# A decoder layer on one core: the samples' decode moved from the chunk loop into the last twelve projection pairs, with q, k and gates stored by chunk

## The chip, the cores and the metric

One Trainium2 chip, one of its cores. The metric is the device time of one execution, in microseconds. Engines: PE is TensorE, DVE is VectorE, ACT is ScalarE, POOL is GpSimd, SP is SyncE, which issues all the DMAs of this kernel.

## The reference

One step of a decoder layer (D = 1024) on 1024 prompt positions and on 8 samples of one position each, all in float32:

```python
x = layer_norm(ALPHA * x + 0.5 * swiglu(x, ffn1_wi, ffn1_wo), ln_g[0], ln_b[0])
z = x @ w_in + b_in
# z is split into q, k, v, o, i, f, B, C, h, gate_a, gate_b; k is scaled by 1/16
h, C, n, m = mlstm_chunkwise(q, k, v, log_i, log_f, C0, n0, m0)   # 4 heads of 256
y_a = (head_norm(h) * sigmoid(o)) @ w_a
y_b = (B * short_conv(C * h)) @ w_b
mix = (sigmoid(gate_a) * y_a + sigmoid(gate_b) * y_b) @ w_mix
x = layer_norm(ALPHA * x + mix, ln_g[1], ln_b[1])
# then a second swiglu with its norm, and a gated per-layer input with its norm
```

The prompt starts from a zero state and runs as eight chunks of 128 positions. Each sample has a state of its own, state_C of 4 heads x 256 x 256: one step of decode is C_new = w C + k v^T, numerator q C_new, denominator q n, both for each of 8 samples and 4 heads; C_new is an output. So the decode reads and writes 8 MB of state.

## The kernel before

All columns (1024 prompt, 8 samples) lie side by side as four blocks of 258: 256 prompt columns, then two samples. A wide matrix product is taken in three float32r products (high weight by high activation, high by low, low by high), with weights of 128x128 and moving tiles of 128x258.

The stages in order of time: the first feed-forward (to some 760 us), the norm, the projections (to some 1509 us), the chunk stage (1500 to 1880 us), the mixing product, the second feed-forward, the gated input.

**Projections.** `pair` (lines 388 to 425) takes 256 output rows by seven products of half-size operands in place of eight. Each product is 12 matmuls for each of two column halves; weights are combined ahead on POOL and DVE and cast by ACT (lines 226 to 243). Its outputs come through a callback `out`: DVE writes a block of 258 columns of d at line 402, 417, 418 or 422, the second index of d telling which of two tiles of 128 rows. `lin` calls it for one head (256 rows) of one of q, k, v, o, gate_b and gate_a. After the whole pair it applies the bias and activation to 1032 columns of each tile in one ACT instruction (line 850), for o a second one with the norm's gain (line 852), and stores the tile to DRAM (line 858). `sg_pair` gives two tiles d in turn from four buffers, so that the pair after can write while the store before runs. The order of calls is convolution, q, k, v of each head, then twelve pairs: o of four heads, gate_b of four, gate_a of four.

**Chunk stage.** For each chunk of 128 positions: scores of 4 heads by transposed operands (lines 1009 and 1017 on PE), state products (lines 157 to 159), the state's update, scaled by ACT at line 1022, the numerator on ACT and DVE (lines 1030 and 1034), its norm over 256 columns on DVE and POOL (lines 981 to 991) and its transposes (line 1059). `chunk_load` (lines 959 to 965) reads q, k and o from DRAM in pieces of 128 columns, 512 bytes each. Work that does not depend on chunks fills it: pieces of w_b and w_a products, with gate data read back at lines 1143 and 1152.

**Decode.** Four steps of one head stand in each chunk. A step (lines 1096 to 1107) loads 256 KB of state into one of two buffers (line 1100), loads v spread over partitions (line 1101), scales the state on ACT (line 1102), adds k v^T in two DVE instructions (line 1104), takes two matmuls into the PSUM tile pn (line 1105, 8 rows of 256) and stores the state (line 1107). After four steps `dec_end` (lines 1109 to 1119) copies pn, normalises it, transposes it and multiplies by the gate. `dec_start` prepares q spread over 8x8 columns (qd) and k scaled (kws).

**Order.** Each engine works through its own list of instructions in order. A scheduler sets the lists from the program's order and its own simulation; the ring of weight tiles and the PSUM tiles (four mm, three aux, one pn) limit how far an engine can run ahead. All DMAs go through SP's one list.

Of the kernel before, what the change touches and what calls it, by code (L numbers as in the profile page):

```python
# [56 lines left out]
def layer_kernel(ctx: ExitStack, tc: tile.TileContext, I, O):  # L57
# [520 lines left out]
    def tail1(RT, last):  # L578
# [10 lines left out]
    x2scr, qscr, kscr, oscr, yscr, ascr, bscr, tbscr, yfscr = (tc.dram_tile([8, 128, NT], F32, name=n) for n in (  # L589
        "x2scr", "qscr", "kscr", "oscr", "yscr", "ascr", "bscr", "tbscr", "yfscr"))  # L590
# [5 lines left out]
    count = {"sg": 0, "w": 0}  # L596
# [318 lines left out]

    conv(0, w0)
    lin(qscr, Q0, 0, AF.Identity, sm=0)
    lin(kscr, K0, 0, AF.Identity, 1.0 / 16.0, 1)
    val(0)
    gates()  # L920
    for h in range(1, 4):
        conv(h)
        lin(qscr, Q0, h, AF.Identity, sm=0)
        lin(kscr, K0, h, AF.Identity, 1.0 / 16.0, 1)
        val(h)
    for h in range(4):
# [3 lines left out]
    for h in range(4):  # L930
        lin(ascr, GA0, h, AF.Sigmoid)


    r_ = ring["slots"][ring["i"] % 9:] + ring["slots"][:ring["i"] % 9]
    big = [i for i in r_ if i in ("e0", "e1", "w4", "w5")]
    small = [i for i in r_ if i not in big]
    set_ring([big[0], small[0], big[1], small[1]])
    QH, QL, KH, KL = ((gen(i, R)[:, :D].rearrange("p (m n) -> p m n", n=128)) for i in small[2:5] + big[2:3])
    EP = gen(big[3])[:, :D]
    S_ = sreg()  # L940
    num = S_[:, 0:NT].rearrange("p (h e) -> p h e", e=258)
    P = S_[:, NT:NT + 512]
    qd = S_[:, NT + 512:NT + 1024].rearrange("p (h t a b) -> p h t a b", h=4, t=2, b=8)
    npc = S_[:, NT + 1024:NT + 1032]
    QC, KC, OC = ([gen(i)[:, :D].rearrange("p (m n) -> p m n", n=128) for i in ii] for ii in ((31, 27), (32, 8), (24, 35)))
    VH, VL = ([gen(i, R).rearrange("p (h e) -> p h e", e=258) for i in ii] for ii in ((25, 9), (26, 30)))
    CX = [t.rearrange("p (h t e) -> p h t e", t=2, e=258)[:, i] for t in (gen(19), gen(33)) for i in range(2)]
    CSH, CSL = [], []
    for i in (34, 29, 20, 21):
        t = gen(i, R).rearrange("p (i t e) -> p i t e", i=2, e=258)  # L950
        CSH.append(t[:, 0])
        CSL.append(t[:, 1])
    PHL = gen(22, R)[:, :D].rearrange("p (i h n) -> p i h n", i=2, n=128)
    CDt = gen(23)[:, :D]
    for i in range(2):
        V.memset(F_(VH[i][:, :, 256:258]), 1.0)
        V.memset(F_(VL[i][:, :, 256:258]), 0.0)

    def chunk_load(c):
        p, cs = c % 2, slice(ccol(c), ccol(c) + 128)  # L960
# [6 lines left out]
    def decay(c):
        e = EP[:, c % 2 * 512:c % 2 * 512 + 512]
        DQ.dma_start(e, bass.AP(tensor=gscr.tensor, offset=gscr.offset + c * 512, ap=[[0, 128], [1, 512]]))
        for h in range(4):  # L970
            eh = e[:, h * 128:(h + 1) * 128]
            V.scalar_tensor_tensor(eh, eh, a_[:, 4 * c + h:4 * c + h + 1], maskb, op0=OP.subtract, op1=OP.max)
        S.activation(e, e, AF.Exp, scale=-1.0)
        return e

    def norm(num_, nr, n, em):
# [89 lines left out]

    kws = cbuf.rearrange("p a b -> p (a b)")[:, 0:64].rearrange("p (h t b) -> p h t b", h=4, t=2)
    ysm = cbuf.rearrange("p a b -> p (a b)")[:, 64:128].rearrange("p (m b) -> p m b", b=8)
    sgn = sg([8, 258], "sgn")
    dn = sg([8, 4], "dn")  # L1070
    dec = {}
    PS = sb.tile([128, 128], R, name="ps_")

    def dec_start():
        t = tmp()
        q8, k8, pr_ = (t[:, 64 * i:64 * i + 64].rearrange("p (h t b) -> p h t b", h=4, t=2) for i in range(3))
        for i, d in enumerate((q8, k8)):
            DQ.dma_start(t[:, 64 * i:64 * i + 64].rearrange("p (m b) -> p m b", b=8), smscr[i].rearrange("m p b -> p m b"))
        e8 = eye8.rearrange("p (a b) -> p a b", b=8)
        for dt in range(2):  # L1080
            wcb, kwb = (wkb[:, :, i, :].rearrange("p b h -> p h b") for i in range(2))
            n_ = nn[:, dt].rearrange("p (b h) -> p h b", h=4)
            V.tensor_tensor(kws[:, :, dt], k8[:, :, dt], kwb, op=OP.mult)
            V.tensor_tensor(n_, n_, wcb, op=OP.mult)
            V.tensor_tensor(n_, n_, kws[:, :, dt], op=OP.add)
            V.tensor_tensor(pr_[:, :, dt], q8[:, :, dt], n_, op=OP.mult)
            for h in range(4):
                V.tensor_tensor(qd[:, h, dt], q8[:, h, dt][:, None, :].to_broadcast([128, 8, 8]), e8, op=OP.mult)
        pd = aux()
        for h in range(4):  # L1090
            for dt in range(2):
                T.matmul(pd[0:8, h:h + 1], pr_[:, h, dt], ones, start=(dt == 0), stop=(dt == 1))
        V.tensor_copy(dn, pd[0:8, 0:4])

    def dec_step(h, s):
        if s % 4 == 0:
            dec["pn"] = psp.tile([128, 512], F32, name="pn", tag="pn", bufs=1)
        cd = CDt[:, (s % 2) * 512:(s % 2) * 512 + 512].rearrange("p (t e) -> p t e", t=2)
        vb = tmp(256)
        DQ.dma_start(cd, I["state_C"][0, s, h].rearrange("(t p) e -> p t e", p=128))  # L1100
        DQ.dma_start(vb, bass.AP(tensor=vscr.tensor, offset=vscr.offset + (h * 8 + s) * 256, ap=[[0, 128], [1, 256]]))
        S.activation(cd, cd, AF.Identity, scale=wkb[:, s, 0, h:h + 1], bias=zer[:, :])
        for dt in range(2):
            V.scalar_tensor_tensor(cd[:, dt], vb, kws[:, h, dt, s:s + 1], cd[:, dt], op0=OP.mult, op1=OP.add)
            T.matmul(dec["pn"][0:8, 0:256], qd[:, h, dt, s], cd[:, dt],  # L1105
                     start=(s % 4 == 0 and dt == 0), stop=(s % 4 == 3 and dt == 1))
        DQ.dma_start(O["C_sample"][0, s, h].rearrange("(t p) e -> p t e", p=128), cd)

    def dec_end(h, u):
        V.tensor_copy(sgn[0:8, 0:256], dec["pn"][0:8, 0:256])  # L1110
        V.tensor_copy(sgn[0:8, 256:257], dn[:, h:h + 1])
        norm(sgn[0:8].rearrange("p (h e) -> p h e", h=1), 8, 1, ems[:, h:h + 1])
        ph = aux()
        for dt in range(2):
            T.transpose(ph[:, dt * 8:dt * 8 + 8], sgn[0:8, dt * 128:(dt + 1) * 128], ident[:8, :8])
        os = tmp(16)
        DQ.dma_start(os.rearrange("p (m b) -> p m b", b=8), smscr[2][2 * h:2 * h + 2].rearrange("m p b -> p m b"))
        os, ph = (x[:, 0:16].rearrange("p (m b) -> p m b", b=8)[:, :, 4 * u:4 * u + 4] for x in (os, ph))
        V.tensor_tensor(ysm[:, 2 * h:2 * h + 2, 4 * u:4 * u + 4], os, ph, op=OP.mult)

# [347 lines left out]
```

## Time and profile before

| | |
|---|---|
| median of 3 runs | 2854.97 us (2854.49 to 2857.7) |
| the profiled execution | 2853.78 us, of it the span 2851.9 us |
| TensorE busy, granted clock | 2757.8 us (97%), 0.986 |
| VectorE, ScalarE, GpSimd busy | 1702.8 us (60%), 1136.2 us (40%), 522.5 us (18%) |
| DMA | 323.89 MB, mean 114 GB/s |

A busy TensorE is one whose matmuls overlap without a gap, so a row's mean duration is longer than the distance from one matmul to the next; what a matmul costs is that distance. The granted clock is the share of full speed that TensorE was given in a stretch. A wait is told as the instruction that waited, the one that released it, and the time its engine was idle.

### The profile page before, as it was taken

Reading aid. Unit: us, or ns where it says so; the run is one execution under the profiler, and the core shown is the slowest. Engines: PE = TensorE matmul, PEld = TensorE weight load, DVE = VectorE, ACT = ScalarE, POOL = GpSimd, SP = SyncE. Lnnn points to the kernel's source line nnn. Section 1 sums busy time; section 2 is a strip of 40 time slices with the busy share of each in tenths; the row PEclk is TensorE's granted clock in tenths of the full one; section 3 lists DMA queues with packets and bytes.
Section 4 is the critical chain, followed back from the end, with each engine's and each line's share of the span. In section 5 each row is a group of like instructions: output and inputs, shape, how many; then the busy total and the mean of one; then the engine's idle time right before and its main releaser. Section 6 shows DMA issues by size and latency. Waiting matters only on the chain.

```text
span 2851.9 us, 52869 instructions
## 1 busy us (share of the span) xinstructions
PE 2757.8 (97%) x20911; PEld 2674.4 (94%) x20911; DVE 1702.8 (60%) x3630; ACT 1136.2 (40%) x2368; POOL 522.5 (18%) x516
## 2 busy tenths in 40 slices
PE   8999999999999999999998998999999999999898
PEld 8999999999899999999997887899999999999776
DVE  7454546555975655645445768748855455654766
ACT  6444444112543444446445444325644444211330
POOL 2111110001430111111101324414311110000533
PEclk9999999999999999999999999999999999999999
DMA  5222227211232233334349877730422224521111
GB/s 193 84 89 75 79 74 255 90 45 34 97 113 68 84 96 98 97 105 126 97 135 275 245 227 219 237 107 20 149 82 82 82 68 135 204 68 57 53 42 54
DMA packets 266739, 323.89 MB, mean 114 GB/s; under 512 B 23441, under 2 KB 212321, under 8 KB 266489
## 3 DMA queue, kind: packets, MB, share of 16 engines
q1 hardware_dynamic: 266488, 320.50, 35.2%
q8 instruction: 164, 2.69, 0.4%
q14 instruction: 87, 0.70, 0.1%
HBM read 230.52 MB, written 89.94 MB: 112 GB/s over the span
## 4 chain that ended last, share of the span: by engine, by line
PE 82%; DVE 8%; DMA 5%; issue 2%; ACT 1%; POOL 1%; SPq 0%; DVEq 0%; ACTq 0%; POOLq 0%
PE mm L384 12%; PE mm L383 12%; PE mm L385 12%; PE mm L157 10%; PE mm L159 10%; PE mm L158 10%; PE aux L384 5%; PE aux L383 5%; PE aux L385 5%; DVE a L193 1%; DMA a<-in_state_C_dram 1%; DVE a L365 1%; DMA e<-gscr 1%; PE pn L1105 1%; DMA a<-yscr 1%
## 5 line engine op out<-in xcount | busy, mean ns | idle before, releaser
L384 PE MATMUL mm<-a,w 128*128 128x258 f32 x1984 | 564.9, 285 | 1.5 <-DVE a L193 1.5
L383 PE MATMUL mm<-a,w 128*128 128x258 f32 x1984 | 561.3, 283 | 1.1 <-DVE a L422 0.7
L385 PE MATMUL mm<-a,w 128*128 128x258 f32 x1984 | 558.2, 281 | 0.0
L159 PE MATMUL mm<-a,w 128*128 128x258 f32 (+2 forms) x1648 | 493.9, 302 | 2.8 <-DVE w L1023 2.2
L157 PE MATMUL mm<-a,w 128*128 128x258 f32 (+2 forms) x1584 | 477.2, 303 | 13.6 <-ACT w L135 6.8
L158 PE MATMUL mm<-a,w 128*128 128x258 f32 (+2 forms) x1584 | 476.5, 302 | 0.3 <-DVE a L193 0.3
L385 PEld LDWEIGHTS mm<-a,w 128*128 128x128 f32 x1984 | 378.5, 191 | 0.0
L384 PEld LDWEIGHTS mm<-a,w 128*128 128x128 f32 x1984 | 375.7, 189 | 2.2 <-DVE a L193 2.2
L383 PEld LDWEIGHTS mm<-a,w 128*128 128x128 f32 x1984 | 373.2, 188 | 1.9 <-DVE a L422 1.0
L159 PEld LDWEIGHTS mm<-a,w 128*128 128x128 f32 x1648 | 313.0, 191 | 5.8 <-DVE w L1023 2.4
L157 PEld LDWEIGHTS mm<-a,w 128*128 128x128 f32 x1584 | 299.7, 190 | 18.5 <-ACT w L135 7.9
L227 DVE TENSOR_TENSOR w<-raw,w 128x512 fp32r<-128x512 f32 x198 | 139.1, 703 | 279.8 <-ACT w L226 275.2
L243 POOL TENSOR_TENSOR raw<-a,raw 128x512 f32<-128x512 f32 x74 | 97.9, 1323 | 1129.7 <-issue 912.8
L158 PEld LDWEIGHTS mm<-a,w 128*128 128x128 f32 x1584 | 300.6, 190 | 1.0 <-DVE a L193 0.5
L502 DVE TENSOR_TENSOR a<-a,mm 128x384 f32<-128x384 f32 (+2 forms) x296 | 147.1, 500 | 171.6 <-PE mm L159 171.2
L384 PE MATMUL aux<-a,w 128*128 128x258 f32 x792 | 226.3, 286 | 0.0
L383 PE MATMUL aux<-a,w 128*128 128x258 f32 x792 | 225.3, 284 | 0.0
L385 PE MATMUL aux<-a,w 128*128 128x258 f32 x792 | 223.6, 282 | 0.0
L384 PE MATMUL mm<-a,e 128*128 128x258 f32 x656 | 186.6, 284 | 0.0
L383 PE MATMUL mm<-a,e 128*128 128x258 f32 x656 | 185.7, 283 | 0.7 <-ACT sreg L405 0.7
L385 PE MATMUL mm<-a,e 128*128 128x258 f32 x656 | 184.7, 282 | 0.0
L226 ACT CAST w<-a 128x512 fp32r<-128x512 f32 x149 | 92.5, 621 | 192.5 <-PE mm L385 103.3
(429 smaller groups left out, 6685.2 us busy)
## 6 DMA issues: line engine op xcount, KB each, us to landing
a<-in_ffn_wi_dram SPq DMA_DIRECT2D x80, 512.0 KB
a<-in_w_in_dram SPq DMA_DIRECT2D x68, 512.0 KB
hscr<-a SPq DMA_DIRECT2D x44, 516.0 KB
a<-hscr SPq DMA_DIRECT2D x44, 516.0 KB
raw<-in_ffn_wo_dram SPq DMA_DIRECT2D x88, 256.0 KB
out_dram<-a SPq DMA_DIRECT2D x34, 256.0 KB
raw<-in_w_b_dram SPq DMA_DIRECT2D x32, 256.0 KB
a<-in_state_C_dram SPq DMA_DIRECT2D x32, 256.0 KB
```

The source lines that it names most:

```text
L157: T.matmul(ps, wh, xh, start=(i == 0), stop=False)
L158: T.matmul(ps, wh, xl, start=False, stop=False)
L159: T.matmul(ps, wl, xh, start=False, stop=(i == n - 1))
L193: V.tensor_tensor(dst[1], src, F_(dst[0]), op=OP.subtract)
L226: S.copy(hi, src)
L227: V.tensor_tensor(lo, src, F_(hi), op=OP.subtract)
L243: G.tensor_tensor(s4, a12, s2, op=OP.subtract)
L365: V.scalar_tensor_tensor(d, d, lng(l, m), y, op0=OP.mult, op1=OP.mult)
L383: T.matmul(ps, wh, xh, start=start and kp == 0, stop=False, skip_group_check=True)
L384: T.matmul(ps, wh, xl, start=False, stop=False, skip_group_check=True)
L385: T.matmul(ps, wl, xh, start=False, stop=stop and kp == 3, skip_group_check=True)
L502: V.tensor_tensor(r, r, ps, op=OP.add)
```

## The change

- `dec_pre`, ahead of the last v pair, does the scaled k, n and the denominator; `dec_start`, ahead of the twelve pairs, spreads q.
- In the twelve pairs `sg_pair` no longer alternates: all use the buffers psgs[0:2], and psgs[2:4] hold qd and three buffers for state. Steps of the decode follow the pairs, three or four a pair after the second to the eleventh. pn now collects eight steps of a head and `dec_end` runs once a head.
- The chunk loop holds chunk, load and filler alone: six filler pieces a chunk in the first four, two in the last four.
- The activation of a pair's output follows block by block inside `out`; for o the norm's gain is multiplied in on POOL.
- The DRAM tiles of q, k and o are laid out by chunk, [8 chunks, 128, 8, 128]. `lin` stores each d in four DMAs of 128 KB, and `chunk_load` reads a chunk of each as whole rows of 4 KB.

```diff
-    x2scr, qscr, kscr, oscr, yscr, ascr, bscr, tbscr, yfscr = (tc.dram_tile([8, 128, NT], F32, name=n) for n in (
+    qscr, kscr, oscr = (tc.dram_tile([8, 128, 8, 128], F32, name=n) for n in ("qscr", "kscr", "oscr"))
...
     def sg_pair():
         i = 2 * (count["sg"] % 2)
-        count["sg"] += 1
+        count["sg"] += count["step"]
...
         def out(i, c, fn):
-            fn(bs(d[i], c, BLK4))
+            k, e = 2 * n + i, bs(d[i], c, BLK4)
+            t = tmp(BW) if dst is oscr else e
+            fn(t)
+            S.activation(t, t, fn_, scale=scale, bias=bcol(c0, k))
+            if dst is oscr:
+                G.tensor_tensor(e, t, gn(k).to_broadcast([128, BW]), op=OP.mult)
...
-            S.activation(d[i], d[i], fn_, scale=scale, bias=bcol(c0, k))
-            if dst is oscr:
-                S.activation(d[i], d[i], AF.Identity, scale=gn(k), bias=zer[:, :])
...
+            if sm is not None:
+                for b in range(4):
+                    DQ.dma_start(dst[2 * b:2 * b + 2, :, k].rearrange("c p n -> p c n"),
+                                 bs(d[i], b, BLK4)[:, 0:256].rearrange("p (c n) -> p c n", n=128))
...
-        DQ.dma_start(KC[p], kscr[:, :, cs].rearrange("m p n -> p m n"))
+        DQ.dma_start(KC[p], kscr[c])
...
+    def dec_start():
+        t = [gen(i) for i in psgs[2:4]]
+        dec["qd"] = qd = t[0][:, 0:512].rearrange("p (h t a b) -> p h t a b", h=4, t=2, b=8)
+        dec["cd"] = [t[0][:, 512:1024], t[1][:, 0:512], t[1][:, 512:1024]]
...
+    if count["sg"] % 2:
+        psgs = psgs[2:] + psgs[:2]
+    count.update(sg=0, step=0)
+    dec_start()
+    for i in range(12):
+        if i < 4:
+            lin(oscr, O0, i, AF.Sigmoid, sm=2)
+        else:
+            lin(*((bscr, GB0) if i < 8 else (ascr, GA0)), i % 4, AF.Sigmoid)
+        for n in range(*(32 * max(0, min(k, 10)) // 10 for k in (i - 1, i))):
+            dec_step(n // 8, n % 8)
+            if n % 8 == 7:
+                dec_end(n // 8)
...
-        for s in range(4):
-            dec_step(c % 4, c // 4 * 4 + s)
-            if c < 4:
-                for f in fill[(4 * c + s) * len(fill) // 16:(4 * c + s + 1) * len(fill) // 16]:
-                    run(f)
-            elif s % 2:
-                run(fill1[2 * (c - 4) + s // 2])
-        dec_end(c % 4, c // 4)
-        if c % 4 == 3:
+        if c % 4 == 0:
             ya_samples(c // 4)
+        for f in fill[6 * c:6 * c + 6] if c < 4 else fill1[2 * c - 8:2 * c - 6]:
+            run(f)
```

TensorE where one chunk of the second half ends and the next begins, before: pn is the decode, line 1059 the transposes after the norm, line 1115 those of the decode's end, lines 1009 and 1017 the next chunk's scores, line 157 the first product of the state.

```order
L1105 MATMUL pn<-a_17878,sreg 8x256
L1059 MATMUL aux<-ident,sreg 128x128 x2
L1105 MATMUL pn<-a_17878,sreg 8x256
L1115 MATMUL aux<-ident,sgn 128x8 x2
L1105 MATMUL pn<-a_17878,sreg 8x256 x2
L1009 MATMUL aux<-a_17862,a_17864 128x128 x8
L1017 MATMUL aux<-ident,a_17864 128x128 x8
L157 MATMUL mm<-a_17868,cd 128x258
```

The same place after (line 1139 is what 1059 was, 1089 and 1097 are 1009 and 1017):

```order
L1139 MATMUL aux<-ident,sreg 128x128 x2
L158 MATMUL mm<-a_18545,w_18527 128x258
L159 MATMUL mm<-a_18545,w_18528 128x258
L1089 MATMUL aux<-a_18534,a_18536 128x128 x8
L1097 MATMUL aux<-ident,a_18536 128x128 x4
L157 MATMUL mm<-a_18545,w_18527 128x258
L158 MATMUL mm<-a_18545,w_18527 128x258
L159 MATMUL mm<-a_18545,w_18528 128x258
L1097 MATMUL aux<-ident,a_18536 128x128 x4
L157 MATMUL mm<-a_18540,cd 128x258
```

The matmuls into pn and the decode's transposes are gone from here, and wide matmuls of the w_a filler stand between transposes and scores.

ScalarE at that place before: line 1102 scales the decode's state, line 1022 the chunk's state, cd.

```order
L1063 CAST a_20141<-a_17866 128x2x128
L1126 CAST a_20137<-cbuf 128x2x2 x2
L1102 ACTIVATE a_17878<-a_17878,zer,wkb 128x512
L1022 ACTIVATE cd<-aux,zer,g_7757 128x256
L1102 ACTIVATE a_17878<-a_17878,zer,wkb 128x512
L192 CAST a_17877<-sreg 128x512
L1022 ACTIVATE cd<-aux,zer,g_7757 128x256 x2
```

ScalarE after, in the seventh of the twelve pairs: line 987 is what 1102 was, line 849 the activation of one block, line 398 a snapshot of a product, line 226 a cast of a weight.

```order
L849 ACTIVATE a_16368<-a_16368,pc 128x258
L987 ACTIVATE a_15195<-a_15195,zer,wkb 128x512
L398 COPY sreg<-mm 128x258 x2
L226 CAST cd<-raw 128x512
L987 ACTIVATE a_15196<-a_15196,zer,wkb 128x512 x2
L849 ACTIVATE a_16632<-a_16632,pc 128x258
L226 CAST w_16944<-a_16927 128x512
L849 ACTIVATE a_16632<-a_16632,pc 128x258
```

The scaling of the state now stands among the blocks of a projection pair, and no longer ahead of cd.

TensorE after, where that pair begins: lines 383 to 385 are a pair's products, line 990 the decode's matmuls. Before, no instruction stood between the products of two pairs.

```order
L384 MATMUL mm<-a_8522,w_16664 128x258
L385 MATMUL mm<-a_8522,w_16664 128x258
L990 MATMUL pn<-a_15195 8x256 x2
L990 MATMUL pn<-a_15196,a_15195 8x256 x4
L383 MATMUL mm<-a_7938,w_16932 128x258
L384 MATMUL mm<-a_7938,w_16932 128x258
```

Six of pn, three steps, stand in a row behind the last product.

SP's list in the gate_b pairs before (line 214 loads weights, line 858 stores d):

```order
L858 DMA bscr<-a_16239 128x1032
L858 DMA bscr<-a_16238 128x1032
L214 DMA a_17166<-in_w_in_dram 128x4x256
L214 DMA a_17395<-in_w_in_dram 128x4x256
L858 DMA bscr<-a_16470 128x1032
L858 DMA bscr<-a_16469 128x1032
L214 DMA a_17397<-in_w_in_dram 128x4x256
L214 DMA a_17626<-in_w_in_dram 128x4x256
```

and after, where line 865 stores d, 985 loads state, 986 loads v and 992 stores state:

```order
L214 DMA a_17456<-in_w_in_dram 128x4x256
L214 DMA a_17737<-in_w_in_dram 128x4x256
L865 DMA bscr<-a_16633 128x1032
L985 DMA a_15195<-in_state_C_dram 128x2x256
L865 DMA bscr<-a_16632 128x1032
L985 DMA a_15196<-in_state_C_dram 128x2x256 x2
L992 DMA out_dram<-a_15195 128x2x256
L986 DMA tmp<-vscr 128x256
L992 DMA out_dram<-a_15196 128x2x256
L986 DMA tmp<-vscr 128x256
```

Between the two stores of a pair now stands a load of state, and behind them the traffic of three steps.

## Rows read from the trace of the kernel before

**Rows 1.** The page's first part: busy time of each engine over the span, its share, instructions.

```profile
PE 2757.8 (97%) x20911; PEld 2674.4 (94%) x20911; DVE 1702.8 (60%) x3630; ACT 1136.2 (40%) x2368; POOL 522.5 (18%) x516
```

**Rows 2.** Busy time by stretch: the last pairs, and the chunk stage in three pieces. Columns: length, then busy time (and instructions) of PE, PEld, DVE, ACT and POOL, then granted clock, DMA share, GB/s.

```profile
1260.00:1500.00 240.00, 240.00 (x2000) 239.96 (x1999) 109.58 (x226) 118.45 (x216) 29.38 (x22) 1.00 0.40 121
1500.00:1655.00 155.00, 136.91 (x983) 117.56 (x983) 106.68 (x288) 75.87 (x142) 40.43 (x34) 0.93 0.85 257
1655.00:1805.00 150.00, 133.43 (x974) 116.56 (x974) 106.72 (x275) 63.11 (x119) 60.15 (x55) 0.95 0.75 222
1805.00:1880.00 75.00, 71.72 (x572) 69.82 (x571) 44.60 (x106) 24.19 (x46) 24.05 (x26) 1.00 0.70 218
```

**Rows 3.** PE's timeline at two places of the chunk stage: start, duration from first start to last end, what, how many merged, and the idle time before it with its releaser.

```profile
1509.76 2.05 PE L1009 MATMUL aux<-a,a 128*128 128x128 f32 x16
1511.65 1.04 PE L1017 MATMUL aux<-ident,a 128*128 128x128 f32 x8
...
1566.95 1.89 PE L1105 MATMUL pn<-a,sreg 128*8 128x256 f32 x8
1568.78 0.39 PE L157 MATMUL mm<-a,e 128*128 128x258 f32 x1
1569.00 0.29 PE L158 MATMUL mm<-a,e 128*128 128x258 f32 x1
```

**Rows 4.** PE's groups by line and form, 1500 to 1880 us: count, busy time, mean ns, idle time before and its releasers.

```profile
L1105 PE MATMUL pn<-a,sreg 128*8 128x256 f32 x128 | 37.6, 424 | 10.4 <-DVE a L1104 8.4 <-DVE sgn L1110 2.0
L1009 PE MATMUL aux<-a,a 128*128 128x128 f32 x128 | 17.1, 288 | 0.0
L1059 PE MATMUL aux<-ident,sreg 128*128 128x128 f32 x64 | 11.9, 283 | 3.9 <-DVE sreg L991 3.9
L1017 PE MATMUL aux<-ident,a 128*128 128x128 f32 x64 | 8.6, 274 | 0.4 <-DVE cbuf L1119 0.4
```

**Rows 5.** Waits from 1500 to 1880 us: who waited for whom, us in total, times, the longest.

```profile
PE mm L157 <- ACT cd L1022: 10.7, 6, 2.9
PE pn L1105 <- DVE a L1104: 8.4, 4, 3.0
```

**Rows 6.** ACT's timeline where three chunks of the second half begin.

```profile
1733.18 0.81 ACT L1102 ACTIVATE a<-a,zer,wkb 128x512 f32<-128x512 f32 x1 [4.20 <-DMA a<-in_state_C_dram]
1733.90 0.55 ACT L1022 ACTIVATE cd<-aux,zer,g 128x256 fp32r<-128x256 f32 x1
...
1767.55 0.81 ACT L1102 ACTIVATE a<-a,zer,wkb 128x512 f32<-128x512 f32 x1 [4.47 <-DMA a<-in_state_C_dram]
...
1800.96 0.81 ACT L1102 ACTIVATE a<-a,zer,wkb 128x512 f32<-128x512 f32 x1 [3.16 <-DMA a<-in_state_C_dram]
```

**Rows 7.** PE's timeline at the first of these places.

```profile
1730.72 1.04 PE L1017 MATMUL aux<-ident,a 128*128 128x128 f32 x8
1734.49 0.39 PE L157 MATMUL mm<-a,cd 128*128 128x258 f32 x1 [2.73 <-ACT cd L1022]
```

**Rows 8.** Busy time by stretch right after the first two of these places, columns as in rows 2.

```profile
1736.00:1740.00 4.00, 4.00 (x12) 1.54 (x10) 3.45 (x8) 3.27 (x7) 0.00 (x0) 0.57 1.15 321
1770.00:1774.00 4.00, 4.00 (x14) 1.76 (x14) 2.84 (x7) 3.26 (x6) 0.00 (x0) 0.57 1.10 350
```

**Rows 9.** One chunk of the second half, busy time as in rows 2; and from DVE's groups of this chunk and the next (1728.8 to 1796.7 us) the decode's.

```profile
1728.80:1762.90 34.10, 29.07 (x207) 24.17 (x206) 27.92 (x70) 15.41 (x31) 15.21 (x14) 0.95 0.82 243
...
L1104 DVE SCALAR_TENSOR_TENSOR a<-tmp,cbuf,a 128x256 f32<-128x256 f32 x18 | 9.9, 587 | 8.6 <-ACT a L1102 8.6
```

**Rows 10.** Groups by line and form: ACT's activations of the projections (1270 to 1500 us), then ACT, POOL and DVE in the chunk stage (1500 to 1880 us).

```profile
L850 ACT ACTIVATE a<-a,pc 128x1032 f32<-128x1032 f32 x22 | 25.4, 1158 | 1.7 <-DVE a L418 1.7
L852 ACT ACTIVATE a<-a,zer,pc 128x1032 f32<-128x1032 f32 x8 | 10.0, 1250 | 0.1
...
L1102 ACT ACTIVATE a<-a,zer,wkb 128x512 f32<-128x512 f32 x32 | 25.7, 814 | 48.6 <-DMA a<-in_state_C_dram 48.5
L1030 ACT ACTIVATE sreg<-mm,zer,g 128x257 f32<-128x257 f32 x28 | 15.7, 562 | 11.2 <-PE mm L159 11.1
L1172 POOL TENSOR_TENSOR a<-a 128x258 f32<-128x258 f32 x32 | 29.8, 937 | 62.8 <-DVE a L1171 24.8 <-DMA a<-tbscr 15.3 <-DVE st L987 15.2
L1104 DVE SCALAR_TENSOR_TENSOR a<-tmp,cbuf,a 128x256 f32<-128x256 f32 x64 | 34.5, 578 | 30.3 <-ACT a L1102 30.3
```

**Rows 11.** SP's timeline from 1268 to 1282 us, the first and the last of sixteen stores of 128 KB (start, time SP spends on issuing, how many); then busy time of that stretch.

```profile
1270.08 0.81 SPq L869 DMA_DIRECT2D vhscr<-tmp  x2
...
1279.73 1.55 SPq L870 DMA_DIRECT2D vlscr<-tmp  x2
...
1268.00:1282.00 14.00, 14.00 (x120) 13.96 (x120) 6.77 (x15) 6.57 (x17) 2.57 (x2) 1.00 0.45 147
```

**Rows 12.** Timelines of DVE, SP and PE around the start of one of the twelve pairs: the last write of d in a pair, the first in the next, the stores of d between them, and the second time that this pair begins a product into aux.

```profile
1428.55 0.42 DVE L422 TENSOR_TENSOR a<-sreg,mm 128x258 f32<-128x258 f32 x1 [1.01 <-PE mm L385]
...
1433.06 0.42 DVE L402 TENSOR_TENSOR a<-sreg,aux 128x258 f32<-128x258 f32 x1
...
1427.66 2.98 SPq L858 DMA_DIRECT2D bscr<-a  x2
...
1437.02 0.28 PE L383 MATMUL aux<-a,w 128*128 128x258 f32 x1
```

More of the change, by code (lines that the diff above doesn't have):

```diff
@@ L930, in layer_kernel @@
[L930 to L948, printed above, removed]
@@ L967, in decay @@
[L967 to L974, printed above, removed]
     def norm(num_, nr, n, em):
@@ new lines, in dec_pre @@
+    def dec_pre():
+        t = tmp()
+        q8, k8 = smp_load(0, t), smp_load(1, t[:, 64:])
+        pr_ = t[:, 128:192].rearrange("p (h t b) -> p h t b", h=4, t=2)
+        for dt in range(2):
+            wcb, kwb = (wkb[:, :, i, :].rearrange("p b h -> p h b") for i in range(2))
+            n_ = nn[:, dt].rearrange("p (b h) -> p h b", h=4)
+            V.tensor_tensor(kws[:, :, dt], k8[:, :, dt], kwb, op=OP.mult)
+            V.tensor_tensor(n_, n_, wcb, op=OP.mult)
+            V.tensor_tensor(n_, n_, kws[:, :, dt], op=OP.add)
+            V.tensor_tensor(pr_[:, :, dt], q8[:, :, dt], n_, op=OP.mult)
+        pd = aux()
+        for h in range(4):
+            for dt in range(2):
+                T.matmul(pd[0:8, h:h + 1], pr_[:, h, dt], ones, start=(dt == 0), stop=(dt == 1))
+        V.tensor_copy(dn, pd[0:8, 0:4])
@@ new lines, in dec_end @@
+    def dec_end(h):
+        V.tensor_copy(sgn[0:8, 0:256], dec["pn"][0:8, 0:256])
+        V.tensor_copy(sgn[0:8, 256:257], dn[:, h:h + 1])
+        norm(sgn[0:8].rearrange("p (h e) -> p h e", h=1), 8, 1, ems[:, h:h + 1])
+        ph = aux()
+        for dt in range(2):
+            T.transpose(ph[:, dt * 8:dt * 8 + 8], sgn[0:8, dt * 128:(dt + 1) * 128], ident[:8, :8])
+        os = tmp(16)
+        DQ.dma_start(os.rearrange("p (m b) -> p m b", b=8), smscr[2][2 * h:2 * h + 2].rearrange("m p b -> p m b"))
+        V.tensor_tensor(ysm[:, 2 * h:2 * h + 2], os.rearrange("p (m b) -> p m b", b=8),
+                        ph[:, 0:16].rearrange("p (m b) -> p m b", b=8), op=OP.mult)
@@ new lines, in layer_kernel @@
+    conv(0, w0)
+    lin(qscr, Q0, 0, AF.Identity, sm=0)
+    lin(kscr, K0, 0, AF.Identity, 1.0 / 16.0, 1)
+    val(0)
+    gates()
+    for h in range(1, 4):
+        conv(h)
+        lin(qscr, Q0, h, AF.Identity, sm=0)
+        lin(kscr, K0, h, AF.Identity, 1.0 / 16.0, 1)
+        if h == 3:
+            dec_pre()
+        val(h)
+    if count["sg"] % 2:
[11 more added lines that the diff above has]
+                dec_end(n // 8)
@@ new lines, in layer_kernel @@
+    r_ = ring["slots"][ring["i"] % 9:] + ring["slots"][:ring["i"] % 9]
+    big = [i for i in r_ if i in ("e0", "e1", "w4", "w5")]
+    small = [i for i in r_ if i not in big]
+    set_ring([big[0], small[0], big[1], small[1]])
+    QH, QL, KH, KL = ((gen(i, R)[:, :D].rearrange("p (m n) -> p m n", n=128)) for i in small[2:5] + big[2:3])
+    EP = gen(big[3])[:, :D]
+    S_ = sreg()
+    num = S_[:, 0:NT].rearrange("p (h e) -> p h e", e=258)
+    P = S_[:, NT:NT + 512]
+    npc = S_[:, NT + 1024:NT + 1032]
@@ new lines, in layer_kernel, with chunk_load, decay @@
+    PHL = gen(22, R)[:, :D].rearrange("p (i h n) -> p i h n", i=2, n=128)
+    for i in range(2):
+        V.memset(F_(VH[i][:, :, 256:258]), 1.0)
+        V.memset(F_(VL[i][:, :, 256:258]), 0.0)
+    def chunk_load(c):
+        p = c % 2
+        DQ.dma_start(KC[p], kscr[c])
+        DQ.dma_start(QC[p], qscr[c])
+        for t, src in ((VH, vhscr), (VL, vlscr)):
+            DQ.dma_start(F_(t[p][:, :, 0:256]), src[:, c].rearrange("h p e -> p h e"))
+        DQ.dma_start(OC[p], oscr[c])
+    def decay(c):
+        e = EP[:, c % 2 * 512:c % 2 * 512 + 512]
+        DQ.dma_start(e, bass.AP(tensor=gscr.tensor, offset=gscr.offset + c * 512, ap=[[0, 128], [1, 512]]))
+        for h in range(4):
+            eh = e[:, h * 128:(h + 1) * 128]
+            V.scalar_tensor_tensor(eh, eh, a_[:, 4 * c + h:4 * c + h + 1], maskb, op0=OP.subtract, op1=OP.max)
+        S.activation(e, e, AF.Exp, scale=-1.0)
+        return e
@@ L1064, in chunk @@
             G.tensor_tensor(yl, y, F_(yh), op=OP.subtract)
[L1067 to L1119, printed above, removed]
```

72 lines of the change are left out of this document (39 added, 33 removed).

## The prediction

> **What bounds the kernel now.** I read the shares of the whole span first: TensorE is busy 97% of it, no other engine over 60% [rows 1]. Time can be won only where TensorE idles, runs at its lower clock or does work that could be left out. So next the same shares by stretch [rows 2]. From 1260 to 1500 us, which holds the last twelve projection pairs, TensorE is busy 240.00 of 240.00 us at granted clock 1.00, with DVE, ACT and POOL at half their time or less. From 1500 to 1880 us, the chunk stage, it idles 18.1 + 16.6 + 3.3 = 38.0 us and the granted clock falls to 0.93 and 0.95.
>
> What the chunk stage needs if TensorE never waits: cadences first. A wide matmul (128x258) costs 240/2000 = 0.120 us [rows 2]. Sixteen 128x128 ones lie 1.89 us ahead of the next instruction, 0.118 each; eight pn matmuls of the decode 1.83 us, 0.229 each [rows 3]. There are 128 pn matmuls and 128 + 64 + 64 of 128x128 [rows 4] among 983 + 974 + 572 = 2529. Need: 128 x 0.229 = 29.3, 256 x 0.118 = 30.2, the other 2145 x 0.120 = 257.4, together 316.9 of 380 us. **Lost: 63.1 us**: 38.0 of idleness, at most 0.07 x 155 + 0.05 x 150 = 18.4 of lower clock, the rest refill after stops.
>
> How much of it is the decode's? Then the waits of this stage [rows 4, 5]: TensorE waits 8.4 + 2.0 us directly at pn. The 10.7 us at line 157 for ACT's cd (line 1022) look like the chunk's own state update. The ACT timeline says otherwise [rows 6]: three times line 1022 stands behind line 1102, the decode's scaling, which waits 4.20, 4.47 and 3.16 us for the state_C load; TensorE then sits idle 2.73 us at line 157 [rows 7]. Three such waits: 8.2 us. After them come stretches of 4 us at granted clock 0.57, some 1.7 us each [rows 8]; with five such places (two are shown) some 8.6 us. Decode's share of the lost time: 8.4 + 2.0 + 8.2 + 8.6 = **27.2 us**.
>
> **Part 1, decode leaves the chunk stage.** Off the path there: 29.3 us of pn and up to 27.2 us of losses, 56.5 us. What is late next is the chunk's own normalisation (line 1059 waits 3.9 us for DVE line 991 [rows 4]) and DVE behind it. In a chunk of the second half DVE is busy 27.92 of 34.10 us; the decode's line 1104 is 9.9 us of two such chunks, 5 us each [rows 9]; its short sgn operations I put at 2 us a chunk. Without them 21 us of work stand in a chunk of some 34 - 56.5/8 = 27 us, 78% as against 82% before: DVE carries it. The state loads, state stores and vb loads (32 x (256 + 256 + 128) KB = 21 MB, 82 us at the stage's 257 GB/s) leave a stage whose DMA share was 0.85 and 0.75; the yscr, gscr and bscr loads can only land earlier. Bounds for the losses given back: 10.4 us (the pn waits alone) to 48.6 (all of 63.1 but the 6.7 of refill and twice the 3.9 of line 1059, which stays and costs clock too). I take 27.2, the sum that rows name.
>
> **Part 2, decode enters the twelve pairs.** TensorE has no gap there, so each pn matmul is paid: +29.3 us. The order shows pn singly among a pair's matmuls in the first three of these pairs and mostly as six in a row after a pair's last product behind them, some 24 places. The wide matmul that follows a bunch starts 0.22 us before its own successor where 0.12 is the cadence [rows 3]; with as much for turning to pn, 0.2 us a place, +4.8 us. The four ends (copy, norm, two transposes, once per head instead of eight times) put transposes amid products behind a DVE chain; nothing shows that place, between 0 and 4 us each with the 2.0 us of the sgn wait [rows 4] in between; with products queued ahead of them I take 1 each, +4. Sum of part 2: **+38.1**, bounds 29.3 to 50. What hides the rest: ACT gets 32 x 0.814 = 26 us of scaling (line 1102), and 96 block activations (128x258) in place of 24 over 1032 columns and of the 10.0 us at line 852 [rows 10]. A 128x257 activation takes 562 ns, so four cost 2.25 us against 1158 ns: +26 - 10. ACT goes from 118 to about 160 of 277 us. DVE gets 34.5 us (line 1104) and some 9 of sgn and qd: 110 to 154. POOL gets 32 multiplications of 128x258 at 0.937 us [rows 10] in place of ACT's: 29 to 59. Every one stays under 60% of a stretch in which TensorE now waits for none of them [rows 2]. The state loads stand in SP's order right behind the previous pair's writes, a pair (20 us) ahead of their pn; the 4 us waits of rows 6 need not follow.
>
> **Part 3, q, k and o by chunk.** A write of 516 KB becomes four of 128 KB for each of 24 rows; a chunk then reads whole rows of 4 KB where it read 512-byte pieces. Such 128 KB writes stand in the trace: sixteen within 11.2 us, in a stretch where TensorE is busy 14.00 of 14.00 us and DMA 0.45 [rows 11]. So I cost them at nothing; their cover is TensorE's own work, and SP's time to issue (0.81 us for two, 72 more) is spread over the pairs. The Trainium skill speaks against this edit: "DMA: Bandwidth & Descriptors", "Rules for kernel authors", wants small transfers coalesced, and "Anatomy of one DMA" there gives each DMA about 2.0 us that no size removes (told for GpSimd's queue; SP issues here). An estimate from that page: 72 more writes, 144 us if one came after the other. Rows 11 show them overlapping, sixteen in the time of less than six such, and nobody waiting; so the sum goes by the row.
>
> **Sum.** -29.3 - 27.2 + 38.1 = **-18.4 us**. The profiled execution took 2853.78 us (its span is 2851.9), 1.2 under the median of 2854.97. So 2835.4 for a run like the profiled one, **2836.6** for the median. With 17 to 37 us given back, or the 38.1 off by as much: 2826 to 2847.
>
> **Rivals.** *More comes back.* The loads of 21 MB and DVE's 7 us a chunk gone, the waits of the normalisation and of the yscr and gscr loads shrink too, and losses fall to 14.5 us: -29.3 - 48.6 + 38.1 = -39.8, 2815. For it: the DMA share was 0.85, its cause leaves. Against: the norm is a serial chain over DVE and POOL, and at such a pace DVE would be over 90% busy.
>
> *The waits change their name.* TensorE's stops at cd and pn hide the chain for the normalisation; without pn and its cover it waits at line 1059 in their place, and only 0 to 15 us come back: -29.3 + 38.1 = +8.8 less these, +8.8 to -6.2, so 2849 to 2864, in the middle 2856. For it: 3.9 us are lost at line 1059 already. Against: the stops named by state_C loads have no other late partner in rows 6 and 7.
>
> *Slower: one pair of buffers for all twelve.* Projections alternate two pairs of d before; after, the second pair holds qd and cd, and each pair of products waits with its first write (DVE, line 402) until the previous bscr or ascr store has landed. In the trace line 422 writes d last at 1428.55, the second store goes out at the end of 1427.66 + 2.98 = 1430.6, and line 402 wants d at 1433.06 [rows 12]. Alone, 516 KB at 257 GB/s take 2.1 us, in time. But now three loads and three stores of 256 KB stand beside it, 2.05 MB, 8.0 us, and a load in front of it waits for six pn (1.4 us): it lands at 1440.0, line 402 is 6.9 us late. aux has three PSUM tiles; the one line 402 frees is asked for 12 matmuls after 1437.02 [rows 12], at 1438.5, which leaves 5.4 us of slack. TensorE would wait 1.5 us and lose 1.7 at the lower clock, eleven times, +35: 2872. It decides from 18.4/11 = 1.7 us a pair. Against: DMA share there is 0.40 and one store needs only its own place in it.
>
> *The small writes hold up the queue.* If the weight loads came late by the issue time of the 72 more writes, 72 x 0.41 = +29 us: 2866. Rows 11 speak against. (By the 2 us of the Trainium skill, "DMA: Bandwidth & Descriptors", "Anatomy of one DMA", it could be more; no row shows it.)
>
> That the change does not do what it says is excluded by the order: no pn stands in the chunk stage any more.
>
> **How the numbers follow.** Forecast 2826 to 2847: 0.61. More comes back (2812 to 2826): 0.13. Waits change their name: 0.12, of it 0.01 faster, 0.10 within 0.2% and 0.01 slower. One pair of buffers 0.12 and small writes 0.02, both slower. A measurement here tells 0.2% (5.7 us) from no change: faster 0.61 + 0.13 + 0.01 = 0.75, same 0.10, slower 0.01 + 0.12 + 0.02 = 0.15. The range leaves out the slower cases and a little at each end: 2812 to 2860.
>
> **What would show it.** In the trace after: the chunk stage is some 324 us long, ACT has no wait for state_C there, granted clock is near 1.00, and TensorE's idle time has gone from 38 to under 22 us, most of it at the transposes after the norm and at yscr and gscr loads. The twelve pairs are 34 to 42 us longer, TensorE without gaps but for a few at the end of a head. If idle time of DVE at line 402's successor ends with a store to bscr or ascr and TensorE has gaps of over a microsecond once a pair, the one pair of buffers was the mistake; if the chunk stage keeps over 50 us of losses, what I put down to the decode was the chain's own.

## The result, and the profile after

The changed kernel takes 2829.34 us (median of 4 runs, 2825.06 to 2830.99) against 2855.19 us before: a ratio of 0.9906, 95% interval 0.9888 to 0.9923, 25.9 us by the medians. The forecast was 2836.6 us, 18.4 less than before, the range 2812 to 2860. (The gates that the title means are o: q, k and o are stored by chunk, gate_a and gate_b as before.) Of all executions below one, the profiled one of the changed kernel without the decode, took 5298.72 us: it is left out of that kernel's time, and no rows of it are shown.

The page's shares after say as little as before [rows 1]: TensorE is still at 97%.

```profile
PE 2751.1 (97%) x20903; PEld 2671.9 (95%) x20903; DVE 1703.8 (60%) x3590; ACT 1158.5 (41%) x2504; POOL 542.5 (19%) x544
```

The stretches tell where the time moved. For this both kernels are cut at the same places: where the first of the twelve pairs begins, where their last product ends, and at a matmul in the second feed-forward from which both run alike. Columns are those of rows 2. Before:

```profile
1264.80:1509.60 244.80, 244.80 (x2049) 244.62 (x2048) 108.72 (x226) 119.29 (x218) 29.84 (x22) 1.00 0.42 129
1509.60:2070.00 560.40, 514.04 (x3813) 473.47 (x3810) 400.08 (x967) 249.41 (x512) 181.06 (x177) 0.96 0.60 182
```

After; the third row is a piece of the second, from the later chunks:

```profile
1266.80:1551.30 284.50, 282.21 (x2172) 256.34 (x2171) 147.29 (x339) 149.26 (x323) 56.15 (x58) 1.00 0.62 186
1551.30:2046.00 494.70, 468.32 (x3658) 458.15 (x3658) 360.46 (x806) 223.85 (x472) 174.95 (x169) 0.98 0.51 163
...
1660.00:1770.00 110.00, 107.34 (x887) 105.69 (x886) 87.58 (x210) 48.67 (x98) 54.23 (x49) 1.00 0.65 209
```

The pairs begin 2.0 us later, take 39.7 us more, and the rest of the way to the mark takes 65.7 us less; behind the mark 781.9 against 781.3 us. Sum: -24.6, the difference of the spans (2827.3 and 2851.9). How far one profile can be trusted, a second one of the changed kernel tells: its pairs begin at 1265.7 us and take 284.3, its stretch to the mark takes 497.0. So the 2.0 us are not all the decode's preparation, which now stands ahead of the pairs, and 2 us in a stretch are noise. In the chunk stage's stretch TensorE idles 26.4 us in place of 46.4, and the granted clock is 0.98 in place of 0.96. DVE carried the faster chunks: 80% busy from 1660 to 1770 us while TensorE ran 107.34 of 110 us at full clock.

TensorE's own waits in the chunk stage after, the longest four (1550 to 1860 us; who waited for whom, us, times, longest). Line 1102 is what 1022 was; its wait was 10.7 us [rows 5], and nothing of the decode is left. The transposes after the norm, which waited 3.9 us [rows 4], wait 0.4:

```profile
PE mm L157 <- ACT cd L1102: 3.0, 5, 1.6
PE mm L157 <- ACT a L192: 2.4, 1, 2.4
PE mm L157 <- ACT w L135: 2.3, 1, 2.3
PE mm L157 <- ACT a L1124: 2.3, 1, 2.3
```

And all engines' waits in the twelve pairs (1264 to 1551 us), the decode's part. ScalarE waits for the state as often, and nearly as long, as it did in the chunk stage (48.5 us [rows 10], in 23 waits there too), but TensorE waits for the decode only twice in the pairs: behind one of its ends (line 1003), and at pn, where VectorE had waited for a load of v and not of the state:

```profile
ACT a L987 <- DMA a<-in_state_C_dram: 43.6, 23, 4.3
DVE a L989 <- ACT a L987: 30.2, 14, 4.9
...
PE aux L383 <- DVE cbuf L1003: 1.2, 1, 1.2
PE pn L990 <- DVE a L989: 0.8, 1, 0.8
```

TensorE's timeline after at the end of a pair, and inside the third pair that holds pn matmuls:

```profile
1407.89 0.28 PE L385 MATMUL mm<-a,w 128*128 128x258 f32 x1
1408.10 1.03 PE L990 MATMUL pn<-a 128*8 128x256 f32 x4
1408.96 1.89 PE L990 MATMUL pn<-a,a 128*8 128x256 f32 x8
1410.78 0.39 PE L383 MATMUL mm<-a,w 128*128 128x258 f32 x1
1411.01 0.28 PE L384 MATMUL mm<-a,w 128*128 128x258 f32 x1
...
1363.76 0.28 PE L384 MATMUL mm<-a,e 128*128 128x258 f32 x1
1364.89 0.60 PE L990 MATMUL pn<-a 128*8 128x256 f32 x2 [0.85 <-DVE a L989]
1365.42 0.39 PE L385 MATMUL mm<-a,e 128*128 128x258 f32 x1
1365.64 0.28 PE L383 MATMUL mm<-a,e 128*128 128x258 f32 x1
```

Three steps in a row (six instructions, twelve records) take 1410.78 - 1408.10 = 2.68 us, 0.223 a record with the turn back. One instruction by itself takes 1365.42 - 1364.89 = 0.53, 0.265 a record. The wait of 0.85 us is the only one of TensorE at pn.

### The profile page after: what moved, and what is told of

It reads as the page before. It is cut to its first block, busy times and chain, and to the rows that moved or that the text cites. A ratio compares the mean times of both kernels' runs of the same rounds, so it can differ in the third digit from the quotient of the medians.

```text
span 2827.3 us, 53142 instructions
## 1 busy us (share of the span) xinstructions
PE 2751.1 (97%) x20903; PEld 2671.9 (95%) x20903; DVE 1703.8 (60%) x3590; ACT 1158.5 (41%) x2504; POOL 542.5 (19%) x544
## 4 chain that ended last, share of the span: by engine, by line
PE 84%; DVE 7%; DMA 4%; ACT 2%; issue 2%; POOL 1%; SPq 0%; DVEq 0%; POOLq 0%; ACTq 0%
PE mm L384 12%; PE mm L383 12%; PE mm L385 12%; PE mm L157 10%; PE mm L159 10%; PE mm L158 10%; PE aux L384 5%; PE aux L383 5%; PE aux L385 5%; DVE a L193 1%; DVE a L365 1%; PE pn L990 1%; DVE a L341 1%; DMA e<-gscr 1%; DVE w L136 0%
## 5 line engine op out<-in xcount | busy, mean ns | idle before, releaser
L157 PEld LDWEIGHTS mm<-a,w 128*128 128x128 f32 x1584 | 298.9, 190 | 15.4 <-ACT w L135 8.5
L135 ACT CAST w<-raw 128x512 fp32r<-128x512 f32 x141 | 85.2, 620 | 179.6 <-PE mm L159 142.5
```

Source lines behind the costliest of these rows:

```text
L135: S.copy(hi, raw)
L157: T.matmul(ps, wh, xh, start=(i == 0), stop=False)
```

## The experiments

Theory: the gain is the decode's place. pn's matmuls take as long at either place; what is won are the stops in the chunk stage. Rivals: the storage by chunk made the chunk stage faster; the waits would only change their name; the one pair of d buffers costs time in the pairs.

**The storage by chunk alone, and the change without it.** On the kernel before:

```diff
+    qscr, kscr, oscr = (tc.dram_tile([8, 128, 8, 128], F32, name=n) for n in ("qscr", "kscr", "oscr"))
...
+                for b in range(4):
+                    DQ.dma_start(dst[2 * b:2 * b + 2, :, k].rearrange("c p n -> p c n"),
+                                 bs(d[i], b, BLK4)[:, 0:256].rearrange("p (c n) -> p c n", n=128))
...
+        DQ.dma_start(KC[p], kscr[c])
...
```

> The kernel before, with q, k and o stored by chunk (four stores of 128 KB in place of one of 516 KB, chunk loads in rows of 4 KB) and nothing else. My theory: the gain is the decode's place; the loads of q, k and o in the chunk stage are not what TensorE waits for, so 2855 us within 6. Rival: the short pieces of these loads were part of why state_C, yscr and gscr loads landed late; then DMA share in the chunk stage falls and at least 8 us come back, 2847 us or less.

Measured 2850.98 us against 2854.65 (0.9988, 0.9979 to 0.9997): some 3 us, inside the theory's range (2849 to 2861) and less than half of the rival's eight. The other way round, the same lines taken out of the changed kernel:

> The changed kernel with q, k and o stored and loaded as before the change, decode and activations as after. My theory: as the changed kernel, 2829 us within 6. Rival (the storage by chunk is worth something once the decode is in the pairs): at least 8 us slower than the changed kernel, 2837 us or more.

Measured 2828.37 us (0.9908, 0.9895 to 0.9922), the changed kernel's own ratio, as the theory had it. So this part may be worth 3 us in the kernel before and is worth nothing that can be told in the new one.

**Block by block activation alone.**

```diff
-            fn(bs(d[i], c, BLK4))
+            k, e = 2 * n + i, bs(d[i], c, BLK4)
+            t = tmp(BW) if dst is oscr else e
+            fn(t)
+            S.activation(t, t, fn_, scale=scale, bias=bcol(c0, k))
+            if dst is oscr:
+                G.tensor_tensor(e, t, gn(k).to_broadcast([128, BW]), op=OP.mult)
...
-            S.activation(d[i], d[i], fn_, scale=scale, bias=bcol(c0, k))
-            if dst is oscr:
-                S.activation(d[i], d[i], AF.Identity, scale=gn(k), bias=zer[:, :])
```

> The kernel before with the projections' activations taken block by block inside the pairs (for o with the gain multiplied in on POOL) and nothing else. My theory: ACT and POOL have the room and TensorE waits for neither in the pairs, so 2855 us within 6. Rival (more ACT instructions delay the weight casts or the snapshots that TensorE waits for): 6 us slower or more, 2861 us up.

Measured 2854.36 us against 2853.82 (1.0005, 0.9996 to 1.0013): nothing, as the theory had it.

**No decode at all, in both kernels.**

```diff
         for s in range(4):
-            dec_step(c % 4, c // 4 * 4 + s)
...
-        dec_end(c % 4, c // 4)
```

> The kernel before without the decode's 32 steps and eight ends (no state load, scaling, update, pn, store; the samples' part of y_a is set to zero, the new states are not written). My theory: the chunk stage gets shorter by the 29.3 us of pn and by the idle and low-clock time that the decode causes, together 57 to 65 us: 2790 to 2798 us. Rival (TensorE's waits only change their name): 29 to 40 us, 2815 to 2826 us.

Measured 2785.45 us (0.9753, 0.974 to 0.9766): the decode costs **69.2 us** in the chunk stage, more than the theory's 57 to 65, and no case for the rival. Its stretches, cut at the same places, and its wait at cd, which was 10.7 us with the decode [rows 5]:

```profile
1263.90:1508.70 244.80, 244.80 (x2048) 244.62 (x2047) 109.57 (x234) 120.24 (x226) 29.85 (x22) 1.00 0.41 127
1508.70:2001.20 492.50, 467.00 (x3669) 456.65 (x3666) 355.00 (x815) 225.55 (x472) 175.24 (x169) 0.99 0.53 165
...
PE mm L157 <- ACT cd L1022: 3.8, 6, 1.9
```

The chunk stage without a decode is 492.5 us to the mark; the changed kernel's is 494.7 (497.0 in its second profile). Moving the decode out has given back all but some 2 to 5 us of what it cost there.

```diff
-        for n in range(*(32 * max(0, min(k, 10)) // 10 for k in (i - 1, i))):
-            dec_step(n // 8, n % 8)
-            if n % 8 == 7:
-                dec_end(n // 8)
```

> The changed kernel without the decode's 32 steps and four ends (left out as in the experiment with the kernel before). My theory: the decode costs 38 to 42 us where it now stands, 30.2 of them pn's own cadence, so 2787 to 2791 us, and the chunk stage is as long as in the changed kernel. Rival (the decode in the pairs also delays what the chunk stage reads, its first loads above all): over 47 us, 2782 us or less, with a shorter chunk stage.

Measured 2786.42 us (median of three executions; 0.9755, 0.974 to 0.977). Against 2829.34 the decode costs **42.9 us** in the pairs, a little over the theory's 38 to 42 and less than the rival's 47; whether the chunk stage is as long as in the changed kernel no row shows. Without decode both kernels take the same time (2785.45 and 2786.42). So nothing else in the change is worth time that can be told, and all that it brings is the decode's price, 69.2 - 42.9 = 26.3 us. That price belongs to the whole move: with its place the decode got four ends in place of eight, pn for eight steps and a third state buffer, and only the buffer is taken back by itself below.

**No loads of state, kernel before.**

```diff
-        DQ.dma_start(cd, I["state_C"][0, s, h].rearrange("(t p) e -> p t e", p=128))
```

> The kernel before with the 32 loads of state_C left out (the decode starts from zeros and its new states are wrong; scaling, update, pn and stores stay). My theory: TensorE's waits at cd behind the decode's scaling, most of those at pn, and the low clock after them go: 18 to 27 us, 2828 to 2837 us. Rival (these waits are ordered by VectorE and the chunk's own chain, the loads only happen to land there): 8 us or less, 2847 us up. 8 MB less for the DMA engines goes with it either way.

Measured 2833.95 us against 2853.82 (0.993, 0.9915 to 0.9945), 19.9 us: the theory's lower end, and more than twice the rival's. TensorE's waits at cd fall from 10.7 to 3.4 us and those at pn from 10.4 to 0.9. The chunk stage's stretch is shorter by 16 us, with less idle time (34.1 us) at a higher clock:

```profile
1508.60:2052.70 544.10, 510.01 (x3811) 474.77 (x3808) 404.09 (x968) 248.02 (x512) 178.25 (x177) 0.97 0.56 172
```

The lists are others too: of ScalarE's 512 instructions in this stretch some 340 stand in the order of the kernel before. So the 19.9 us are the loads with the 8 MB and the new order, not the waits by themselves.

**No pn, in both kernels.**

```diff
-            T.matmul(dec["pn"][0:8, 0:256], qd[:, h, dt, s], cd[:, dt],
-                     start=(s % 4 == 0 and dt == 0), stop=(s % 4 == 3 and dt == 1))
```

> The kernel before without the decode's 64 matmuls into pn (the samples' numerator is a constant; loads, scaling, update, stores and the ends stay). My theory: besides the 29.3 us of cadence go the turns to pn and back (5 us), the idle time at pn (10.4 us) and part of the low clock after it: 45 to 52 us, 2802 to 2810 us, and with the 20 us of the experiment without loads nearly the whole 69 us of the decode is named. Rival (all losses hang on the loads and on ScalarE's scaling): 29 to 35 us, 2819 us up.

Measured 2842.02 us against 2853.59 (0.9952, 0.9937 to 0.9966): **11.6 us**, less than pn's own cadence. Both theories fall. TensorE does 29 us less and waits more, for others (1506 to 1880 us; the profiled execution, 2836.22 us, is the fastest of its four):

```profile
ACT a L1100 <- DMA a<-in_state_C_dram: 55.9, 21, 6.4
PE mm L157 <- ACT a L192: 9.3, 5, 7.3
PE mm L157 <- DVE a L1155: 8.1, 4, 4.0
PE mm L157 <- ACT cd L1022: 6.1, 6, 2.4
```

Its stretch has 60.5 us of idle time where the kernel before has 46.4, at a lower clock:

```profile
1506.20:2053.60 547.40, 486.94 (x3687) 470.95 (x3684) 402.66 (x973) 249.00 (x512) 179.07 (x177) 0.95 0.61 187
```

> The changed kernel without the 64 matmuls into pn (left out as in the kernel before). My theory: in the pairs pn is nearly all that the decode costs, 27.6 us of cadence, 5 of turns and 1 to 3 of waits, so 33 to 37 us, 2792 to 2796 us. Rival (loads, scaling and stores cost TensorE time there too): under 30 us, 2799 us up.

Measured 2814.93 us (0.9856, 0.9838 to 0.9873) against 2830.3 for the changed kernel run beside it: **15.4 us** for a predicted 33 to 37, so by the number it is the rival's case (under 30). In the profiled execution, again the fastest of four (2806.97 us), the pairs are 268.5 us long in place of 284.5, and TensorE, which hardly idled there, now idles 15.8 us:

```profile
1262.50:1531.00 268.50, 252.75 (x2043) 249.09 (x2042) 147.25 (x339) 144.94 (x323) 56.23 (x58) 0.99 0.65 197
```

The waits in its pairs (1284 to 1531 us) name two ways to get there: VectorE's first write of d waits for the store of the pair before, and a snapshot on ScalarE (line 398) stands behind a scaling that waits for its state load:

```profile
ACT a L985 <- DMA a<-in_state_C_dram: 21.9, 16, 3.7
...
DVE a L402 <- DMA bscr<-a: 11.9, 4, 3.5
...
PE mm L383 <- ACT sreg L398: 5.4, 3, 3.1
```

In the changed kernel the same place looks like this (ScalarE's timeline; on TensorE the pn of the pair before start at 1433.04 us, the next product at 1435.73):

```profile
1437.02 0.81 ACT L987 ACTIVATE a<-a,zer,wkb 128x512 f32<-128x512 f32 x1 [2.33 <-DMA a<-in_state_C_dram]
1437.74 0.35 ACT L398 COPY sreg<-mm 128x258 f32<-128x258 f32 x1
1438.98 0.38 ACT L398 COPY sreg<-mm 128x258 f32<-128x258 f32 x1 [0.89 <-PE mm L385]
```

The scaling waits 2.33 us, and yet it is the second snapshot that waits for TensorE (0.89 us) and not the other way: six pn in front of the pair have moved its products by 2.6 us. So at this place pn covers a wait of the rest of the decode. The scheduler made new lists for both kernels (of TensorE's 2041 other matmuls in the pairs some 1530 stand in the order of the changed kernel), so how much of the missing 18 to 22 us is such cover and how much the new order stays open.

**One pair of d for the twelve pairs, kernel before.**

```diff
-        count["sg"] += 1
+        count["sg"] += count["step"]
...
+    count["step"] = 0
     for h in range(4):
         lin(oscr, O0, h, AF.Sigmoid, sm=2)
```

> The kernel before with one pair of d tiles for all twelve last pairs, no alternation, nothing else moved. My theory: the stores of d land before the next pair writes d, or late by less than the spare PSUM tile covers, so 2855 us within 6. Rival, the slower case of the prediction: TensorE waits 1.5 us a pair and pays 1.7 at the lower clock, 2872 us or more.

Measured 2853.81 us against 2853.82 (0.9998, 0.999 to 1.0006). The mechanism is there and its price is not. VectorE waits 14.2 us in nine waits, and one wait of TensorE follows:

```profile
DVE a L402 <- DMA ascr<-a: 6.2, 3, 4.3
DVE a L402 <- DMA bscr<-a: 5.2, 4, 2.3
DVE a L402 <- DMA oscr<-a: 2.8, 2, 2.1
...
PE aux L383 <- DVE a L402: 0.6, 1, 0.6
```

The rest is covered; that the third PSUM tile does it, as the prediction reckoned, is likely and not shown. The rival's traffic of state beside the stores is not in this run, but it is in the changed kernel, and there no such wait is listed at all. Without pn the changed kernel has them (11.9 us for bscr above), which points to the six pn ahead of the next pair as what gives the store its time.

**Two state buffers in place of three, changed kernel.**

```diff
-        dec["cd"] = [t[0][:, 512:1024], t[1][:, 0:512], t[1][:, 512:1024]]
+        dec["cd"] = [t[0][:, 512:1024], t[1][:, 0:512]]
...
-        cd = dec["cd"][(8 * h + s) % 3].rearrange("p (t e) -> p t e", t=2)
+        cd = dec["cd"][s % 2].rearrange("p (t e) -> p t e", t=2)
```

> The changed kernel with two state buffers in place of three. My theory: the third buffer is what lets the loads of a pair's steps go out a pair ahead; with two, one step in three is loaded in the pair that uses it and TensorE waits at pn, 5 to 25 us: 2834 to 2854 us. Rival (the products queued ahead cover a load of 4 us wherever it stands): 2829 us within 4.

> The changed kernel itself, as the base for the others of this call: 2829 us within 4.

Measured 2826.5 us (0.99, 0.9884 to 0.9917), and 2830.3 us for the changed kernel again (0.9913, 0.9899 to 0.9928). My theory falls, and the time is inside the rival's range: TensorE waits 1.9 us at pn in place of 5 to 25. The pairs do get longer, but the chunk stage is shorter by as much.

```profile
1265.10:1555.30 290.20, 286.17 (x2172) 255.96 (x2171) 145.85 (x339) 147.44 (x322) 55.96 (x58) 1.00 0.60 182
1555.30:2043.90 488.60, 466.02 (x3659) 455.98 (x3658) 359.20 (x806) 224.48 (x474) 173.29 (x169) 0.99 0.52 166
```

No line of the edit touches the chunk stage, whose 488.6 us stand beside 494.7 and 497.0 of the changed kernel's two profiles. The scheduler's order has changed with it: of TensorE's 3656 matmuls in that stretch some 3510 stand in the changed kernel's order, while its two profiles agree in all. The intervals overlap, so this is not shown to be the faster kernel.

**Filler ahead of the first chunk, changed kernel.**

```diff
+    for f in fill[0:2]:
+        run(f)
     for c in range(8):
...
-        for f in fill[6 * c:6 * c + 6] if c < 4 else fill1[2 * c - 8:2 * c - 6]:
+        for f in fill[2 + 22 * c // 4:2 + 22 * (c + 1) // 4] if c < 4 else fill1[2 * c - 8:2 * c - 6]:
```

> The changed kernel with two filler pieces (w_b products) called ahead of the first chunk, the other 22 spread over the first four. My theory: TensorE's gaps at the start of the chunk stage, where the first chunk has no other work beside it (1.75, 2.42 and 2.56 us, and 6.9 us at half clock after them), are filled: 4 to 9 us faster than the changed kernel, 2820 to 2825 us. Rival (the filler's own loads and casts are as late there as the chunk's): 2829 us within 4.

Measured 2833.81 us against 2853.82 (0.993, 0.9918 to 0.9943), no faster than the changed kernel. My theory falls; the rival's range ends 0.8 us below, and its reason shows: from 1549 to 1580 us TensorE still idles 5.4 us where the changed kernel idles 6.5, now mostly ahead of filler products that wait for their own casts (lines 192 and 193). Up to the mark it idles 29.6 us (26.4 in the changed kernel), and its longest waits (1549 to 1900 us) have other names:

```profile
PE aux L1139 <- DVE sreg L938: 3.2, 2, 2.5
PE mm L157 <- DVE a L1121: 2.7, 1, 2.7
PE mm L157 <- DVE a L1183: 2.3, 2, 2.0
```

## Why the prediction was right, step by step

- *Where time can be won.* Right. The chunk stage's idle time and clock were the decode's to a large part: of 46.4 us of idle time 25.5 stay without a decode (492.50 - 467.00), 20.9 go.
- *Decode's share of the losses, 27.2 us.* Near, by both its parts. Idle time gave 20.0 us (I had 8.4 + 2.0 + 8.2 = 18.6). For the clock the hundredths of the rows are too coarse: the stretches at half clock (1.2 GHz) add up to 41.0 us before and 20.5 after, and what they took from a busy TensorE is 17.3 and 8.9 us, so 8.4 came back (I had 8.6).
- *The term that was mis-sized* is one that I put at nothing. In the stretch to the mark the change took 65.7 us: 29.3 of pn, 20.0, 8.4, and 8.0 more, in which TensorE was busy at full clock. Adding up the distances from start to start, pn itself is 30.3 us, the sixteen transposes of the decode's ends are 1.8, and the matmuls that stay take some 4 less: they follow one another more closely where there is no stop and no turn to pn. I had called such time refill, 6.7 us, and left it out of what can come back, and I charged turns in the pairs and forgot that as many leave the chunk stage. It is most of the 9.2 us by which part 1 fell short (65.7 for 56.5).
- *Part 2, +38.1.* Measured +39.7, in part by two errors that offset each other. pn and its turns cost more: 30.2 us for pn and 6.8 more for the wide matmuls, mostly at the 27 places where pn stands between them, 37.0 where I had 34.1. The ends cost less: 0.9 us for their transposes and no more than the 2.3 of all idle time where I had 4. The 16 matmuls of the preparation, which I had not moved, are half a microsecond ahead of the pairs. That pn is all that is paid and the rest is hidden does not hold as I put it: without pn the rest costs 28.5 us (2814.93 - 2786.42), in a kernel with other lists; both together cost 42.9.
- *"The 4 us waits need not follow."* ScalarE's did: it waits 43.6 us for state_C, 23 times. What I had missed is that the scaling stands close behind its load, and only pn stands a pair behind both. For one bunch the loads go out at 1410.2, 1410.9 and 1417.9 us, the scalings start at 1415.10, 1416.08 and 1422.41, and their pn at 1433.04. So TensorE meets the state long after ScalarE's wait. That what else is on ScalarE's list comes in time too is seen from TensorE's 2.3 us of idle time in the pairs.
- *Part 3 at nothing.* Right in the new kernel. Against it I had weighed the rule of the Trainium skill ("DMA: Bandwidth & Descriptors", "Rules for kernel authors") to coalesce small transfers. Here 72 more stores cost no time that can be told (2829.34 us with, 2828.37 without).
- *What would show it.* The pairs are 39.7 us longer, as said, and no wait for state_C is left in the chunk stage. But the idle time that stays is not at the transposes after the norm (0.4 us): it stands before line 157, for ScalarE's casts and the scaling of cd.
- *Rivals.* More came back than forecast, but not to the 14.5 us of losses of the first rival. The waits did not change their name where the whole decode left; they did where pn alone was taken out. The slower case had its mechanism and not its price.

## What to carry to other kernels

Take the whole suspect out once, at its old and its new place: 69.2 and 42.9 us told at once what moving it is worth, where taking out single parts (19.9 and 11.6 us) did not add up to the whole. The small matmuls themselves took as long at either place (30.3 and 30.2 us at full clock); what was won by moving this chain of load, scaling, update and matmul is the stops that it made on engines whose lists also hold the critical work, and the low clock after them. So put such a chain where the bounding engine has other work queued, and its last step well behind the first. Where a scheduler writes the lists, an edit can reorder stages that it does not touch (488.6 against 494.7 us here): compare the lists, and put no difference of that size down to the edit.

## What the runs showed of the hardware that was not expected

A float32 matmul of 8 x 256 is one instruction in the lists (64 into pn) and two records in the trace (128), of 0.216 us each in a row, against 0.120 us for a float32r one of 128 x 258. Turning from a wide matmul to pn takes 0.21 us from start to start (1407.89 to 1408.10) where two wide ones lie 0.12 apart; the way back is 0.31 us from the last pn to the wide one, and 0.23 from that to the next (1410.78 to 1411.01). Together a bunch of pn costs some 0.3 us beyond its own matmuls.
